# A shared tail, scaling on GpSimd and a second load behind a memset, in a ReLU-and-mean kernel

## Chip, cores and metric

The kernel runs on one core of one Trainium2 chip. The metric is the device time of one execution in microseconds (us). A time below is a median of several executions unless it says otherwise.

## The reference

```python
x = np.random.randn(32, 512, 1024).astype(np.float32)
def reference(x):
    return np.mean(np.maximum(x, 0), axis=-1).astype(np.float32)
```

There are 16,384 rows of 1024 floats (67.1 MB) to read, and one mean for each row to write (64 KB).

## The kernel before

Each of the 128 partitions holds J = 128 rows, in eight tiles of 16 rows (8.39 MB each). Three buffers take the tiles in turn. Seven tiles are loaded whole. The eighth comes in pieces of 8, 4, 2 and 1 rows, and its last row in pieces of 512, 256 and 256 columns, so that the work left over after the last bytes is small. Odd rows go to VectorE (DVE), even rows to ScalarE (ACT); each takes the ReLU and sums the row in one instruction of the kernel (1.22 us on DVE, 1.04 on ACT for 1024 columns in the trace, where the read of the accumulator follows it as an operation of its own, of 0.08 and 0.19 us).

```python
def rows(xt, lo, n, j0):
    for k in range(lo, lo + n):
        j = j0 + k
        if j % 2: dve_row(nc, xt[:, k, :], sum_v[:, j:j + 1])
        else:     act_row(nc, xt[:, k, :], sum_a[:, j:j + 1])

def finish(lo, hi):                    # scaling by 1/D, half on each engine
    nc.vector.tensor_scalar_mul(out=res[:, lo + 1:hi:2], in0=sum_v[:, lo + 1:hi:2], scalar1=inv)
    nc.scalar.mul(out=res[:, lo:hi:2], in_=sum_a[:, lo:hi:2], mul=inv)

for t in range(full):                  # full = 7
    xt = in_pool.tile([P, NB, D], F32, name="xt")
    nc.sync.dma_start(out=xt, in_=xr[:, j0:j0 + NB, :])
    rows(xt, 0, NB, j0)
# ... cut: the pieces of the eighth tile, finish() ...
act_row(nc, xt[:, lo, :D // 2], part_a[:, 0:1])          # row 14 of the last tile
dve_row(nc, xt[:, lo, D // 2:], part_v[:, 0:1])
act_row(nc, last[:, :D // 4], part_a[:, 1:2])            # row 15
dve_row(nc, last[:, D // 4:D // 2], part_v[:, 1:2])
nc.vector.tensor_scalar(...)                             # row 14: add the halves, scale
dve_row(nc, last[:, D // 2:3 * D // 4], part_v[:, 2:3])
nc.vector.tensor_scalar(...)                             # row 15: add three parts
dve_row(nc, last[:, 3 * D // 4:], part_v[:, 3:4])
nc.vector.tensor_scalar(...)                             # row 15: add the fourth, scale
nc.sync.dma_start(out=outr, in_=res)
```

Of the kernel before, what the change touches and what calls it, by code (L numbers as in the profile page):

```python
# [1 line left out]

# [4 lines left out]

F32 = mybir.dt.float32
ALU = mybir.AluOpType
RELU = mybir.ActivationFunctionType.Relu  # L10


def act_row(nc, src, acc):

    nc.scalar.activation(out=src, in_=src, func=RELU, accum_out=acc)  # L15


def dve_row(nc, src, acc):

    nc.vector.tensor_scalar(  # L20
        out=src, in0=src, scalar1=0.0, scalar2=None,
        op0=ALU.max, op1=ALU.add, accum_out=acc,
    )


@with_exitstack
def kernel(
    ctx: ExitStack,
    tc: tile.TileContext,
    x: bass.AP,  # L30
    out: bass.AP,
):
    nc = tc.nc
    P = nc.NUM_PARTITIONS
    xf = x.flatten_outer_dims()
    R, D = xf.shape
    assert R % P == 0
    J = R // P
    inv = 1.0 / D
    xr = xf.rearrange("(p j) d -> p j d", p=P, j=J)  # L40
    outr = out.flatten().rearrange("(p j) -> p j", p=P, j=J)

    NB = 16
    BUFS = 3
    full = J // NB - 1

    row_pieces = []
    left = NB
    while left > 1:
        row_pieces.append(left // 2)  # L50
        left -= left // 2
    col_pieces = [D // 2, D // 4, D // 4]

    in_pool = ctx.enter_context(tc.tile_pool(name="in", bufs=BUFS))
    res_pool = ctx.enter_context(tc.tile_pool(name="res", bufs=1))
    sum_a = res_pool.tile([P, J], F32)
    sum_v = res_pool.tile([P, J], F32)
    res = res_pool.tile([P, J], F32)
    part_a = res_pool.tile([P, 2], F32)
    part_v = res_pool.tile([P, 4], F32)  # L60

    def rows(xt, lo, n, j0):

        for k in range(lo, lo + n):
            j = j0 + k
            if j % 2:
                dve_row(nc, xt[:, k, :], sum_v[:, j:j + 1])
            else:
                act_row(nc, xt[:, k, :], sum_a[:, j:j + 1])

    def finish(lo, hi):

        nc.vector.tensor_scalar_mul(out=res[:, lo + 1:hi:2], in0=sum_v[:, lo + 1:hi:2], scalar1=inv)  # L73
        nc.scalar.mul(out=res[:, lo:hi:2], in_=sum_a[:, lo:hi:2], mul=inv)  # L74

    for t in range(full):
        j0 = t * NB
        xt = in_pool.tile([P, NB, D], F32, name="xt")
        nc.sync.dma_start(out=xt, in_=xr[:, j0:j0 + NB, :])  # L79
        rows(xt, 0, NB, j0)  # L80

    j0 = full * NB
    xt = in_pool.tile([P, NB, D], F32, name="xt")
    lo = 0
    for n in row_pieces:
        nc.sync.dma_start(out=xt[:, lo:lo + n, :], in_=xr[:, j0 + lo:j0 + lo + n, :])  # L86
        lo += n
    c = 0
    for w in col_pieces:
        nc.sync.dma_start(out=xt[:, lo, c:c + w], in_=xr[:, j0 + lo, c:c + w])  # L90
        c += w

    finish(0, j0)
    lo = 0
    for n in row_pieces[:-1]:
        rows(xt, lo, n, j0)
        lo += n
    finish(j0, j0 + lo)


    last = xt[:, NB - 1, :]
    act_row(nc, xt[:, lo, :D // 2], part_a[:, 0:1])
    dve_row(nc, xt[:, lo, D // 2:], part_v[:, 0:1])
    act_row(nc, last[:, :D // 4], part_a[:, 1:2])
    dve_row(nc, last[:, D // 4:D // 2], part_v[:, 1:2])
    nc.vector.tensor_scalar(  # L106
        out=res[:, J - 2:J - 1], in0=part_a[:, 0:1], scalar1=part_v[:, 0:1], scalar2=inv,
        op0=ALU.add, op1=ALU.mult,
    )
    dve_row(nc, last[:, D // 2:3 * D // 4], part_v[:, 2:3])  # L110
    nc.vector.tensor_scalar(  # L111
        out=part_v[:, 1:2], in0=part_v[:, 1:2], scalar1=part_a[:, 1:2], scalar2=part_v[:, 2:3],
        op0=ALU.add, op1=ALU.add,
    )
    dve_row(nc, last[:, 3 * D // 4:], part_v[:, 3:4])
    nc.vector.tensor_scalar(  # L116
        out=res[:, J - 1:J], in0=part_v[:, 3:4], scalar1=part_v[:, 1:2], scalar2=inv,
        op0=ALU.add, op1=ALU.mult,
    )
    nc.sync.dma_start(out=outr, in_=res)  # L120


# [1 line left out]
_INS = ['x']  # L124
_OUTS = [((32, 512), 'float32')]


# [23 lines left out]
```

## Time and profile before

| | before |
|---|---|
| time, median of the first 3 runs | 164.88 us |
| span in the profile | 163.1 us |
| DMA queue of the loads, share of 16 engines | 96.0% |
| DVE / ACT busy | 46% / 43% |
| first tile landed | 23.2 us |
| last piece landed | 159.19 us |
| end of DVE's last operation | 160.61 us |

A load "lands" with the last of the 16 completion marks that the trace has for it. The time from the last landing to the end of DVE's last operation I call the tail: 1.42 us here. After it come the store (1.6 us from issue to landing) and the end of the program. The views give the last landing to a tenth of a microsecond: the issue of the last piece in the timeline (its start is 120.16 us), then its size and its time from issue to landing in the DMA view. The second digit is from the marks themselves.

```profile
120.16 0.33 SPq L90 DMA_DIRECT2D xt<-in_x_dram  x1
xt<-in_x_dram SPq DMA_DIRECT2D x1, 128.0 KB, 39.0
```

Two lines of the page of the kernel before give busy shares and the chain of work that ended last:

```profile
DVE 75.4 (46%) x139; ACT 69.4 (43%) x133; POOL 0.2 (0%) x4
...
DMA 83%; DVE 14%; SPq 1%; issue 0%; DVEq 0%
```

The compute engines are idle over half of the time, and the chain is loads. The windows view of the same kernel tells why no change of compute can move much. Its columns are the stretch, its length, busy time of DVE, ACT and GpSimd (POOL), the clock, the DMA share and GB/s (a packet counts where it starts):

```profile
1.40:2.30 0.90, 0.00 (x0) 0.61 (x1) 0.00 (x0) 1.00 2.25 728
2.30:3.40 1.10, 0.00 (x0) 0.00 (x0) 0.00 (x0) 1.00 1.04 357
...
10.00:90.00 80.00, 36.25 (x63) 33.69 (x64) 0.00 (x0) 1.00 1.00 434
```

From 10 to 90 us the loads run at 434 GB/s.

The tail is read from the timeline (start, duration, engine, line, operation):

```profile
157.88 0.17 DVE L73 TENSOR_SCALAR res<-sum_v 128x7 f32<-128x7 f32 x1
157.91 0.63 ACT L15 ACTIVATE xt<-xt 128x512 f32<-128x512 f32 x1
157.96 0.68 DVE L20 TENSOR_SCALAR_CACHE_REDUCE xt<-xt 128x512 f32<-128x512 f32 x1
...
158.75 0.21 DVE L106 TENSOR_SCALAR res<-part_a,part_v 128x1 f32<-128x1 f32 x1
158.87 0.19 ACT L15 ACTIVATION_READ_ACCUMULATOR xt<-xt 128x1 f32 x1
158.88 0.41 DVE L20 TENSOR_SCALAR_CACHE_REDUCE xt<-xt 128x256 f32<-128x256 f32 x1
...
159.22 0.42 DVE L20 TENSOR_SCALAR_CACHE_REDUCE xt<-xt 128x256 f32<-128x256 f32 x1
...
159.75 0.27 DVE L111 TENSOR_SCALAR part_v<-part_v,part_a 128x1 f32<-128x1 f32 x1
159.94 0.41 DVE L20 TENSOR_SCALAR_CACHE_REDUCE xt<-xt 128x256 f32<-128x256 f32 x1
160.27 0.08 DVE L20 DVE_READ_ACCUMULATOR xt<-xt 128x1 f32 x1
160.39 0.21 DVE L116 TENSOR_SCALAR res<-part_v 128x1 f32<-128x1 f32 x1
```

ACT is done at 159.06. DVE goes on for 1.5 us, and its last piece, landed at 159.19, is not begun before 159.94. The combinations of single numbers (lines 106, 111, 116) cost 0.21 to 0.27 us each, half of a 256-column sum or more.

### The profile page before, as it was taken

The numbers are of one execution on the slowest core, as the hardware profiler recorded it, in microseconds if no ns is written. First come the engines' busy times: TensorE is split into PE (matmuls) and PEld (weight loads), VectorE is DVE, ScalarE is ACT, GpSimd is POOL, SyncE is SP. The second block draws the span as 40 slices with busy tenths as digits, with TensorE's granted clock in tenths as the row PEclk, the third lists the DMA queues.
The fourth block names the chain that finished last, engine by engine and source line by source line (L and its number), as shares of the span: only waits on it lengthen the run. The fifth ranks groups of instructions, "written<-read, shape, count | busy, mean of one in ns | idle before, by whom it ended". The sixth has DMA issues, their size and how long they took to land.

```text
span 163.1 us, 351 instructions
## 1 busy us (share of the span) xinstructions
DVE 75.4 (46%) x139; ACT 69.4 (43%) x133; POOL 0.2 (0%) x4
## 2 busy tenths in 40 slices
DVE  0000039900596008940099202990059700799993
ACT  3000039700594008920099002980059500797890
POOL 0000000000000000000000000000000000000000
DMA  7979989989998998997997998998998897999970
GB/s 257 482 321 482 482 354 450 514 354 418 514 418 354 514 418 354 514 482 305 498 484 340 466 498 354 434 514 370 402 514 386 386 514 338 434 442 394 409 298 16
DMA packets 2162, 67.19 MB, mean 412 GB/s; under 512 B 240, under 2 KB 624, under 8 KB 880
## 3 DMA queue, kind: packets, MB, share of 16 engines
q1 hardware_dynamic: 2160, 67.18, 96.0%
q14 instruction: 2, 0.02, 0.0%
HBM read 67.11 MB, written 0.07 MB: 412 GB/s over the span
## 4 chain that ended last, share of the span: by engine, by line
DMA 83%; DVE 14%; SPq 1%; issue 0%; DVEq 0%
DMA xt<-in_x_dram 83%; DVE xt L20 13%; SPq L86 0%; SPq L79 0%; DVE part_v L111 0%; DVE res L116 0%; DVE res L106 0%; DVE res L73 0%; DVEq L20 0%; DVEq L111 0%; DVEq L106 0%
## 5 line engine op out<-in xcount | busy, mean ns | idle before, releaser
L20 DVE TENSOR_SCALAR_CACHE_REDUCE xt<-xt 128x1024 f32<-128x1024 f32 (+1 forms) x67 | 74.4, 1172 | 84.9 <-DMA xt<-in_x_dram 84.8
L15 ACT ACTIVATE xt<-xt 128x1024 f32<-128x1024 f32 (+1 forms) x65 | 66.7, 1027 | 88.9 <-DMA xt<-in_x_dram 88.9
L15 ACT ACTIVATION_READ_ACCUMULATOR xt<-xt 128x1 f32 x65 | 12.1, 187 | 0.0
L20 DVE DVE_READ_ACCUMULATOR xt<-xt 128x1 f32 x67 | 5.6, 83 | 0.0
L15 ACT ACT_TABLE_LOAD x1 | 1.3, 1283 | 0.7 <-PEq L135 0.7
L74 ACT ACTIVATE res<-sum_a 128x56 f32<-128x56 f32 (+1 forms) x2 | 0.5, 232 | 0.1
L73 DVE TENSOR_SCALAR res<-sum_v 128x56 f32<-128x56 f32 (+1 forms) x2 | 0.4, 184 | 0.1
L111 DVE TENSOR_SCALAR part_v<-part_v,part_a 128x1 f32<-128x1 f32 x1 | 0.3, 273 | 0.1
L106 DVE TENSOR_SCALAR res<-part_a,part_v 128x1 f32<-128x1 f32 x1 | 0.2, 214 | 0.1
L116 DVE TENSOR_SCALAR res<-part_v 128x1 f32<-128x1 f32 x1 | 0.2, 214 | 0.0
L135 POOL MEMSET const-uint8-127<- 128x1 uint8 x1 | 0.1, 102 | 0.0
L135 POOL MEMSET const-bfloat16-1.0<- 128x1 bf16 x1 | 0.1, 101 | 0.0
L135 POOL MEMSET const-float32-0.0<- 128x1 f32 x1 | 0.1, 98 | 0.2 <-issue 0.2
L135 POOL MEMSET const-float32-1.0<- 128x1 f32 x1 | 0.1, 98 | 0.0
## 6 DMA issues: line engine op xcount, KB each, us to landing
xt<-in_x_dram SPq DMA_DIRECT2D x1, 4096.0 KB, 39.0
xt<-in_x_dram SPq DMA_DIRECT2D x1, 2048.0 KB, 43.5
xt<-in_x_dram SPq DMA_DIRECT2D x1, 1024.0 KB, 45.5
xt<-in_x_dram SPq DMA_DIRECT2D x1, 512.0 KB, 46.3
xt<-in_x_dram SPq DMA_DIRECT2D x1, 256.0 KB, 46.5
xt<-in_x_dram SPq DMA_DIRECT2D x2, 128.0 KB, 42.7
xt<-in_x_dram SPq DMA_DIRECT2D x7, 48.9
out_dram<-res SPq DMA_DIRECT2D x1, 64.0 KB, 1.6
```

What stands on the lines that cost most here:

```text
L15: nc.scalar.activation(out=src, in_=src, func=RELU, accum_out=acc)
L20: nc.vector.tensor_scalar(out=src, in0=src, scalar1=0.0, scalar2=None, op0=ALU.max, op1=ALU.add, accum_out=acc,)
L73: nc.vector.tensor_scalar_mul(out=res[:, lo + 1:hi:2], in0=sum_v[:, lo + 1:hi:2], scalar1=inv)
L74: nc.scalar.mul(out=res[:, lo:hi:2], in_=sum_a[:, lo:hi:2], mul=inv)
L106: nc.vector.tensor_scalar(out=res[:, J - 2:J - 1], in0=part_a[:, 0:1], scalar1=part_v[:, 0:1], scalar2=inv, op0=ALU.add, op1=ALU.mult,)
L111: nc.vector.tensor_scalar(out=part_v[:, 1:2], in0=part_v[:, 1:2], scalar1=part_a[:, 1:2], scalar2=part_v[:, 2:3], op0=ALU.add, op1=ALU.add,)
L116: nc.vector.tensor_scalar(out=res[:, J - 1:J], in0=part_v[:, 3:4], scalar1=part_v[:, 1:2], scalar2=inv, op0=ALU.add, op1=ALU.mult,)
L135: nc = _bacc.Bacc("TRN2", target_bir_lowering=False, num_devices=1)
```

## The change

It wants to shorten the tail and to order the start. (1) The scaling and the combination of row 14 go to GpSimd. (2) In the third quarter of row 15, ACT takes 128 columns. DVE's last two sums take the sum before them as start value instead of being added later, and ACT folds in its own parts while DVE works on the last piece. (3) The second load is issued only after GpSimd has set two rows of its buffer to zero. The core of the diff (cut: names, constants, the merging of the sum tiles):

```diff
-def dve_row(nc, src, acc):
+def dve_row(nc, src, acc, init=None):
-        out=src, in0=src, scalar1=0.0, scalar2=None,
+        out=src, in0=src, scalar1=0.0, scalar2=init,
...
-        nc.vector.tensor_scalar_mul(out=res[:, lo + 1:hi:2], ...)
-        nc.scalar.mul(out=res[:, lo:hi:2], ...)
+        nc.gpsimd.tensor_scalar(out=res[:, lo:hi], in0=sums[:, lo:hi], scalar1=inv, scalar2=0.0, ...)
...
+        if t == 1:
+            nc.gpsimd.memset(xt[:, 0:2, :], 0.0)
...
-    nc.vector.tensor_scalar(out=res[:, J - 2:J - 1], ...)
+    nc.gpsimd.tensor_scalar(out=res[:, J - 2:J - 1], ...)
-    dve_row(nc, last[:, D // 2:3 * D // 4], part_v[:, 2:3])
-    nc.vector.tensor_scalar(out=part_v[:, 1:2], ...)
-    dve_row(nc, last[:, 3 * D // 4:], part_v[:, 3:4])
-    nc.vector.tensor_scalar(out=res[:, J - 1:J], ...)
+    nc.gpsimd.tensor_scalar(out=part[:, 4:5], in0=part[:, 2:3], scalar1=inv, ...)
+    act_row(nc, last[:, 512:640], part[:, 5:6])
+    dve_row(nc, last[:, 640:768], part[:, 6:7], init=part[:, 3:4])
+    nc.scalar.activation(out=part[:, 7:8], in_=part[:, 5:6], func=ACT.Identity, scale=inv, bias=part[:, 4:5])
+    dve_row(nc, last[:, 768:], part[:, 8:9], init=part[:, 6:7])
+    nc.vector.scalar_tensor_tensor(out=res[:, J - 1:J], in0=part[:, 8:9], scalar=inv, in1=part[:, 7:8], ...)
```

More of the change, by code (lines that the diff above doesn't have):

```diff
@@ L9 @@
 ALU = mybir.AluOpType
-RELU = mybir.ActivationFunctionType.Relu
+ACT = mybir.ActivationFunctionType
 def act_row(nc, src, acc):
-    nc.scalar.activation(out=src, in_=src, func=RELU, accum_out=acc)
-def dve_row(nc, src, acc):
+    nc.scalar.activation(out=src, in_=src, func=ACT.Relu, accum_out=acc)
+def dve_row(nc, src, acc, init=None):
     nc.vector.tensor_scalar(
-        out=src, in0=src, scalar1=0.0, scalar2=None,
+        out=src, in0=src, scalar1=0.0, scalar2=init,
         op0=ALU.max, op1=ALU.add, accum_out=acc,
@@ L41 @@
     outr = out.flatten().rearrange("(p j) -> p j", p=P, j=J)
+    xlast = xr[:, J - 1, :]
     NB = 16
-    BUFS = 3
     full = J // NB - 1
-    row_pieces = []
-    left = NB
-    while left > 1:
-        row_pieces.append(left // 2)
-        left -= left // 2
-    col_pieces = [D // 2, D // 4, D // 4]
-    in_pool = ctx.enter_context(tc.tile_pool(name="in", bufs=BUFS))
+    row_pieces = [8, 4, 2, 1]
+    assert sum(row_pieces) == NB - 1
+    col_pieces = [512, 256, 256]
+    assert sum(col_pieces) == D
+    in_pool = ctx.enter_context(tc.tile_pool(name="in", bufs=3))
     res_pool = ctx.enter_context(tc.tile_pool(name="res", bufs=1))
-    sum_a = res_pool.tile([P, J], F32)
-    sum_v = res_pool.tile([P, J], F32)
+    sums = res_pool.tile([P, J], F32)
     res = res_pool.tile([P, J], F32)
-    part_a = res_pool.tile([P, 2], F32)
-    part_v = res_pool.tile([P, 4], F32)
+    part = res_pool.tile([P, 10], F32)
     def rows(xt, lo, n, j0):
@@ L65, in rows @@
             j = j0 + k
-            if j % 2:
-                dve_row(nc, xt[:, k, :], sum_v[:, j:j + 1])
-            else:
-                act_row(nc, xt[:, k, :], sum_a[:, j:j + 1])
+            (dve_row if j % 2 else act_row)(nc, xt[:, k, :], sums[:, j:j + 1])
     def finish(lo, hi):
-        nc.vector.tensor_scalar_mul(out=res[:, lo + 1:hi:2], in0=sum_v[:, lo + 1:hi:2], scalar1=inv)
-        nc.scalar.mul(out=res[:, lo:hi:2], in_=sum_a[:, lo:hi:2], mul=inv)
+        nc.gpsimd.tensor_scalar(
+            out=res[:, lo:hi], in0=sums[:, lo:hi], scalar1=inv, scalar2=0.0, op0=ALU.mult, op1=ALU.add,
+        )
     for t in range(full):
@@ L83 @@
     xt = in_pool.tile([P, NB, D], F32, name="xt")
+    prev, last = xt[:, NB - 2, :], xt[:, NB - 1, :]
     lo = 0
@@ L89 @@
     for w in col_pieces:
-        nc.sync.dma_start(out=xt[:, lo, c:c + w], in_=xr[:, j0 + lo, c:c + w])
+        nc.sync.dma_start(out=last[:, c:c + w], in_=xlast[:, c:c + w])
         c += w
@@ L98 @@
     finish(j0, j0 + lo)
-    last = xt[:, NB - 1, :]
-    act_row(nc, xt[:, lo, :D // 2], part_a[:, 0:1])
-    dve_row(nc, xt[:, lo, D // 2:], part_v[:, 0:1])
-    act_row(nc, last[:, :D // 4], part_a[:, 1:2])
-    dve_row(nc, last[:, D // 4:D // 2], part_v[:, 1:2])
-    nc.vector.tensor_scalar(
-        out=res[:, J - 2:J - 1], in0=part_a[:, 0:1], scalar1=part_v[:, 0:1], scalar2=inv,
-        op0=ALU.add, op1=ALU.mult,
-    )
-    dve_row(nc, last[:, D // 2:3 * D // 4], part_v[:, 2:3])
-    nc.vector.tensor_scalar(
-        out=part_v[:, 1:2], in0=part_v[:, 1:2], scalar1=part_a[:, 1:2], scalar2=part_v[:, 2:3],
-        op0=ALU.add, op1=ALU.add,
-    )
-    dve_row(nc, last[:, 3 * D // 4:], part_v[:, 3:4])
-    nc.vector.tensor_scalar(
-        out=res[:, J - 1:J], in0=part_v[:, 3:4], scalar1=part_v[:, 1:2], scalar2=inv,
-        op0=ALU.add, op1=ALU.mult,
+    act_row(nc, prev[:, :512], part[:, 0:1])
+    dve_row(nc, prev[:, 512:], part[:, 1:2])
+    nc.gpsimd.tensor_scalar(
+        out=res[:, J - 2:J - 1], in0=part[:, 0:1], scalar1=part[:, 1:2], scalar2=inv, op0=ALU.add, op1=ALU.mult,
+    )
+    act_row(nc, last[:, :256], part[:, 2:3])
+    dve_row(nc, last[:, 256:512], part[:, 3:4])
+    nc.gpsimd.tensor_scalar(
+        out=part[:, 4:5], in0=part[:, 2:3], scalar1=inv, scalar2=0.0, op0=ALU.mult, op1=ALU.add,
+    )
+    act_row(nc, last[:, 512:640], part[:, 5:6])
+    dve_row(nc, last[:, 640:768], part[:, 6:7], init=part[:, 3:4])
+    nc.scalar.activation(
+        out=part[:, 7:8], in_=part[:, 5:6], func=ACT.Identity, scale=inv, bias=part[:, 4:5],
+    )
+    dve_row(nc, last[:, 768:], part[:, 8:9], init=part[:, 6:7])
+    nc.vector.scalar_tensor_tensor(
+        out=res[:, J - 1:J], in0=part[:, 8:9], scalar=inv, in1=part[:, 7:8], op0=ALU.mult, op1=ALU.add,
     )
```

## The prediction

> **What bounds the kernel now.** The load stream. The page gives DMA 96% of 16 engines' span, DVE 46%, ACT 43%; the chain of waits is 83% DMA, 14% DVE. From issue times plus issue-to-landing times, the seven full tiles land at 23.2, 42.5, ... 139.6 us, one per 19.3 to 19.4 us; 8.39 MB in 19.35 us is 433 GB/s. [...] What can move is the start (issue 0.73, first landing 23.2: about 3 us more than a steady tile) and the tail.
>
> **Tail before (timeline).** The last pieces land at about 156.6 (rows 12, 13), 157.8 (row 14), 158.5, 158.85 and 159.16 us (row 15). DVE, not the last load, ends the chain: row 13 from 156.62, scaling 157.88, half row, 158.75 combination (0.21), 256 columns at 158.88 and 159.22, combination of 0.27, 256 columns at 159.94, last combination 160.39 to 160.60. Then the store (1.6 us) and the end.
>
> **What the change does to the tail.** It takes the scaling (0.17) and two combinations (0.21, 0.27) off DVE and gives 128 of its columns to ACT (a 256-column op costs DVE 0.41, ACT 0.42; 512 columns 0.68 and 0.63; so I estimate 128 columns at 0.28 and 0.31). In exchange two DVE ops now take the preceding DVE sum as their start value: each waits for the accumulator read and a semaphore (0.11 us gap, as the trace shows before the 0.27 us combination) and carries a pointer operand (+0.04 to 0.06, from 0.21 and 0.27 against 0.17). My schedule: half row to 158.5; 256 columns from 158.56 (their landing); 128 from 159.1; last 256 from 159.55 to 160.0; final op 160.13 to 160.4. DVE gains only about 0.2 us. ACT: 128 columns to 159.4, then Identity; it needs a GpSimd product that can start at about 159.15. [...] no table load; the trace's ACT scaling after Relu has none either. GpSimd has about 0.5 us before it delays DVE; no GpSimd arithmetic is in the trace, only 0.1 us memsets, so this is my weakest size.
>
> **What the memset does.** 128x2048 floats on GpSimd[...] hold loads 2 and 3 back [...]. Load 1 occupies the engines until about 21 us, so nothing starves. In the trace eight engines' first packets start at 1.6 to 2.1 us, the other eight only at 2.4 to 3.0, after issue of load 2 at 1.16, and this stagger survives to the end. If the second issue causes it, delaying it brings the late engines forward by up to 0.8 us, and all landings with them. I give that less than even odds: worth 0.2 us in the mean.
>
> **Sum.** 164.88 - 0.2 (tail) - 0.2 (start) = 164.45 us. Range 163.7 to 165.2. Faster by over 2% would need 3.3 us, more than tail and start hold; slower by over 2% needs a table load plus slow GpSimd ops.
>
> **What would show it.** Landings still 19.3 to 19.4 us apart; first landing 23.2 (no effect) or 22.4 to 23.0 (stagger gone); no second table load; DVE's last op ending 1.2 us after the last landing instead of 1.44; [...] loads 2, 3 issued behind it.
>
> **What would make it wrong.** GpSimd ops of 1 us or more, making the last combination wait for ACT's Identity, or the store for GpSimd; a larger gain at the start; the delayed issue slowing the stream, for instance if loads must be queued early to follow on without a gap; the pointer start value costing DVE more than I took.

Sum: it takes 0.2 us for the tail and 0.2 us for the start off 164.88 us and was put at 164.45 us (164.48 without a slip).

## The result and the profile after

The changed kernel took 164.81 us (median of 4 runs, 164.4 to 164.86) beside 164.94 us for the kernel before (4 runs). The ratio is 0.9984, with a 95% interval of 0.9964 to 1.0004. A ratio here and below is the mean time of one kernel's fast runs over that of the kernel before in the same rounds, so it is not quite the ratio of the medians. With more rounds the changed kernel came out at 0.9976 (0.9959 to 0.9994), so it is about 0.4 us faster (0.1 to 0.7 us by the interval).

The page after, the same two lines:

```profile
DVE 74.7 (46%) x135; ACT 69.6 (43%) x134; POOL 3.0 (2%) x9
...
DMA 83%; DVE 13%; POOL 1%; SPq 1%; issue 0%; DVEq 0%; POOLq 0%
```

The loads are still the chain. The 1% of POOL in it is the memset at the start, through which the trace now leads back to the second load. The windows of the same stretches:

```profile
1.40:2.30 0.90, 0.00 (x0) 0.61 (x1) 0.90 (x1) 1.00 2.25 728
2.30:3.40 1.10, 0.00 (x0) 0.00 (x0) 0.24 (x1) 1.00 0.99 357
...
10.00:90.00 80.00, 36.16 (x63) 33.70 (x64) 0.00 (x0) 1.00 1.01 434
```

Again ten first packets start before 2.3 us and six after it, and the rate is the same 434 GB/s. The tail in the timeline after:

```profile
158.33 0.69 DVE L20 TENSOR_SCALAR_CACHE_REDUCE xt<-xt 128x512 f32<-128x512 f32 x1
158.43 0.22 POOL L65 TENSOR_SCALAR res<-sums 128x14 f32<-128x14 f32 x1 [8.71 <-DVE xt L20]
...
158.96 0.42 DVE L20 TENSOR_SCALAR_CACHE_REDUCE xt<-xt 128x256 f32<-128x256 f32 x1
159.20 0.27 POOL L101 TENSOR_SCALAR res<-part 128x1 f32<-128x1 f32 x1 [0.55 <-ACT xt L15]
...
159.31 0.08 DVE L20 DVE_READ_ACCUMULATOR xt<-xt 128x1 f32 x1
...
159.43 0.35 DVE L20 TENSOR_SCALAR_CACHE_REDUCE xt<-xt,part 128x128 f32<-128x128 f32 x1
159.55 0.19 POOL L106 TENSOR_SCALAR part<-part 128x1 f32<-128x1 f32 x1
...
159.81 0.48 DVE L20 TENSOR_SCALAR_CACHE_REDUCE xt<-xt,part 128x256 f32<-128x256 f32 x1
159.86 0.29 ACT L111 ACTIVATE part<-part 128x1 f32<-128x1 f32 x1
160.22 0.08 DVE L20 DVE_READ_ACCUMULATOR xt<-xt,part 128x1 f32 x1
160.41 0.16 DVE L115 SCALAR_TENSOR_TENSOR res<-part 128x1 f32<-128x1 f32 x1
```

The same two views of the last piece after:

```profile
120.57 0.33 SPq L87 DMA_DIRECT2D xt<-in_x_dram  x1
xt<-in_x_dram SPq DMA_DIRECT2D x1, 128.0 KB, 39.0
```

In this trace the last piece landed at 159.60 us, 0.41 us later than in the trace of before, and DVE ended at 160.57, 0.04 us earlier. So the tail fell from 1.42 to 0.97 us, and nearly all of that gain is hidden by a later landing. Either the memset caused the later landing, or it was chance.

### The profile page after: what moved, and what is told of

It reads as the page before. It is cut to its first block, busy times and chain, and to the rows that moved or that the text cites. A ratio compares the mean times of both kernels' runs of the same rounds, so it can differ in the third digit from the quotient of the medians.

```text
span 163.1 us, 361 instructions
## 1 busy us (share of the span) xinstructions
DVE 74.7 (46%) x135; ACT 69.6 (43%) x134; POOL 3.0 (2%) x9
## 4 chain that ended last, share of the span: by engine, by line
DMA 83%; DVE 13%; POOL 1%; SPq 1%; issue 0%; DVEq 0%; POOLq 0%
DMA xt<-in_x_dram 83%; DVE xt L20 12%; POOL xt L74 1%; SPq L83 1%; DVE res L115 0%; DVEq L20 0%; SPq L75 0%; DVEq L115 0%; POOLq L133 0%
## 5 line engine op out<-in xcount | busy, mean ns | idle before, releaser
L65 POOL TENSOR_SCALAR res<-sums 128x112 f32<-128x112 f32 (+1 forms) x2 | 0.5, 254 | 155.6 <-DVE xt L20 155.6
L74 POOL MEMSET xt<- 128x2048 f32 x1 | 1.8, 1805 | 0.3 <-POOLq L133 0.3
L20 DVE TENSOR_SCALAR_CACHE_REDUCE xt<-xt,part 128x128 f32<-128x128 f32 (+1 forms) x2 | 0.8, 412 | 0.1
```

The costliest lines, as they stand in the source:

```text
L20: nc.vector.tensor_scalar(out=src, in0=src, scalar1=0.0, scalar2=init, op0=ALU.max, op1=ALU.add, accum_out=acc,)
L65: nc.gpsimd.tensor_scalar(out=res[:, lo:hi], in0=sums[:, lo:hi], scalar1=inv, scalar2=0.0, op0=ALU.mult, op1=ALU.add,)
L74: nc.gpsimd.memset(xt[:, 0:2, :], 0.0)
```

## The experiments

Theory H1 was: the tail is worth 0.45 us, the memset nothing, and the later landing of the one trace is chance. The rival H2 was: holding the second load back makes the stream end later and eats the gain. The first four runs separate the parts of the change, beside a control, on one chip.

### Control: the kernel before, unchanged

> A null control: the kernel before, unchanged. 164.9 us, ratio 1.000 within 0.001 under every theory. It gives the spread that a difference of 0.3 us has to stand out from. In its trace: where the last load lands (159.2 us in the first trace of before) and how far apart the 16 completions of one load lie (0.95 us, then 1.17 us after about 90 us). If the last landing moves by 0.3 us or more here, landings of one trace can't be read as an effect of the change.

Measured: 165.15 us (6 runs), ratio 0.9996 (0.9977 to 1.0015). Its last landing was at 159.65 us, against 159.19 in the first trace of the same program. So a landing in one trace varies by 0.46 us with nothing changed. That is as much as the difference that H2 was built on. Its tail was 1.43 us. The 16 completion marks of one load lay 0.90 and 0.87 us apart for its first two tiles, 1.21 us from the third on and 1.75 us from the fifth on. Both steps are tiles that landed late, 19.73 and 19.87 us after the tile before.

### The changed kernel again

> The changed kernel again. Theory H1 (the tail is 0.45 us shorter, the memset worth nothing, and the later last landing of its first trace, 159.6 against 159.2 us, was chance): about 164.5 us, ratio 0.997 to 0.998. Rival H2 (the held-back second load makes the stream end 0.4 us later and eats the tail's gain): ratio 0.9985 to 1.000, and the last landing again at about 159.6 us.

Measured: 164.72 us (6 runs), ratio 0.9976 (0.9959 to 0.9994), last landing 159.30 us, tail 0.97 us. The landing did not repeat at 159.6, against H2.

### The memset alone

```diff
         xt = in_pool.tile([P, NB, D], F32, name="xt")
+        if t == 1:
+            nc.gpsimd.memset(xt[:, 0:2, :], 0.0)
         nc.sync.dma_start(out=xt, in_=xr[:, j0:j0 + NB, :])
```

> The kernel before with only the memset of the second buffer. H1: ratio 1.000, no effect beyond the control's spread. H2: 165.3 us, ratio 1.002 to 1.003, last landing about 159.6 us. Under both the second load is issued at about 2.55 us in place of 1.16.

Measured: 165.09 us (5 runs), ratio 1.0001 (0.9982 to 1.002), last landing 159.23 us, tail 1.43 us. The memset alone is worth nothing that these rounds can see. H1 holds so far.

### The tail alone

```diff
-        if t == 1:
-            nc.gpsimd.memset(xt[:, 0:2, :], 0.0)
```

> The changed kernel without the memset: only the tail. H1: the same as the changed kernel, ratio 0.997 to 0.998. H2: faster than the changed kernel by 0.3 to 0.4 us, ratio 0.9965 to 0.9975 while the changed kernel is at 0.9985 to 1.000. Under both, DVE's last operation ends about 0.97 us after the last landing, against 1.42 us before.

Measured: 164.54 us (5 runs), ratio 0.9967 (0.9949 to 0.9986), tail 0.97 us. Its interval overlaps that of the changed kernel (0.9959 to 0.9994), so it can't be ranked against it. Together with the run before, this puts the gain in the tail. H2 falls: the memset alone did not come out at 1.002 to 1.003 (its interval just reaches 1.002), and in three more traces with a held load (the changed kernel again, the memset alone, the hold below) the last piece landed at 159.2 to 159.3 us and not at 159.6. A cost of 0.1 or 0.2 us of the memset is not excluded by these times.

### Holding the second load eight times as long

```diff
-            nc.gpsimd.memset(xt[:, 0:2, :], 0.0)
+            nc.gpsimd.memset(xt, 0.0)
```

> The changed kernel with the memset over the whole second buffer, 8 times the work: by the 1.805 us measured for one eighth it should take 14.4 us and hold load 2 back to about 15.2 us. H1 (a held-back load costs nothing while the load before it still feeds the DMA engines): time unchanged, 164.3 to 164.9 us, first landing 23.1 us and 19.3 to 19.5 us between landings. Rival (loads must be queued early, or any hold costs some of the stream): slower by 0.5 us or more, with the gap between the first and the second landing above 19.5 us.

Measured: 164.52 us (4 runs), ratio 0.9964 (0.995 to 0.9977). The timeline has the memset and the two loads held behind it (SPq is the DMA issue of SyncE):

```profile
0.73 13.75 POOL L74 MEMSET xt<- 128x16384 f32 x1 [0.29 <-POOLq L133]
...
14.51 0.81 SPq L75 DMA_DIRECT2D xt<-in_x_dram  x2
```

The second load is issued 13.35 us later than in the kernel before (1.16 us), and the second landing comes 19.31 us after the first, as before. A load held while another still ran cost nothing here.

### Holding it twice as long again

```diff
             nc.gpsimd.memset(xt, 0.0)
+            nc.gpsimd.memset(xt, 0.0)
```

> The changed kernel with that whole-buffer memset twice: load 2 issued at about 29.6 us, after load 1 has landed at 23.1. Under H1 this is where the hold must start to cost: the second landing comes the first load's own 22.4 us after the issue, at about 52.0 us in place of 42.4, and the whole program is 9.5 us longer, about 174 us (173 to 175). If the time moves by much less than 8 us, I have the order of the loads or their queueing wrong.

My expectation failed: 164.66 us (4 runs), ratio 0.9973 (0.9958 to 0.9988). The trace shows why. Two loads were issued at once (0.74 and 1.16 us) and only the third waited for GpSimd, until 28.32 us. In the built program the unheld load stands ahead of the held one; I take this to be the work of the tile scheduler, which no run tested. The held load was not needed before the second landing at 42.6 us. This run says nothing of a hold beyond the first load's end, so the experiment was built anew.

### Holding loads 2 and 3 beyond the end of load 1

```diff
+    scr = res_pool.tile([P, 2048], F32)
+    for _ in range(15):
+        nc.gpsimd.memset(scr, 0.0)
...
-        if t == 1:
-            nc.gpsimd.memset(xt[:, 0:2, :], 0.0)
+        if t in (1, 2):
+            nc.gpsimd.tensor_copy(out=xt[:, 0, 0:1], in_=scr[:, 0:1])
```

> The changed kernel with loads 2 and 3 both held back behind 15 GpSimd memsets of 128x2048 on a scratch tile (a one-column copy from that tile into each buffer makes the dependence): load 2 issued at about 28.5 to 29.5 us, 5 to 6 us after load 1 has landed. The run with two memsets on one buffer did not do this, since the tile scheduler moved the third load ahead of the held one. H1: now the DMA engines stand idle from about 22 to 30 us, the second landing comes 21.3 to 22.4 us after the issue, at 50 to 52 us in place of 42.45, and all that follows is 8 to 9.5 us later: 172.5 to 174 us. Rival (the stream catches up later): less than 168 us.

Measured: 173.61 us (4 runs), ratio 1.0511. The windows show the hole in the stream (last column GB/s), and the waits of the DMA issue name GpSimd:

```profile
20.00:23.00 3.00, 0.00 (x0) 0.00 (x0) 2.94 (x2) 1.00 0.20 87
23.00:30.00 7.00, 6.92 (x13) 6.92 (x13) 5.73 (x6) 1.00 0.18 56
30.00:40.00 10.00, 2.28 (x5) 1.50 (x4) 0.00 (x0) 1.00 0.92 380
```

```profile
SPq L78 <- POOL xt L77: 27.9, 1, 27.9
```

The issue came at 28.87 us and the second landing 28.10 us after the first instead of 19.3. Nothing of these 8.8 us is caught up later: the time is 8.9 us over the 164.72 us of the changed kernel (on another chip). So the changed kernel's hold to 2.56 us is free because the first load keeps the DMA engines fed until about 22 us (in this trace the last of its packets start at 20.3 us and end at 22.7 us). If a later issue costs one for one, 28.87 less 8.8 puts the limit of a free hold near 20 us; that is an estimate from this one run.

### Which part of the tail gained

Two builds add the parts of the new tail to the kernel before, one after the other. First the scaling on GpSimd:

```diff
-        nc.vector.tensor_scalar_mul(out=res[:, lo + 1:hi:2], ...)
-        nc.scalar.mul(out=res[:, lo:hi:2], ...)
+        for first, s in ((lo, sum_a), (lo + 1, sum_v)):
+            nc.gpsimd.tensor_scalar(out=res[:, first:hi:2], in0=s[:, first:hi:2], scalar1=inv, ...)
```

> The kernel before with only the final scaling (the two operations of 0.17 and 0.21 us at rows 112 to 125) moved to GpSimd. I read the tail in the trace, since its length from the last landing to the end of DVE's last operation came out the same within 0.02 us in every run so far: 1.42 to 1.43 us before, 0.97 to 0.99 after. DVE's half row started 0.08 us after row 14 landed because of the scaling, so I expect 1.35 us (1.30 to 1.43). If the scaling were the larger part of the gain, the tail would be near 1.1 us.

Measured: tail 1.38 us (one run of 165.01 us). Then also the combination of row 14:

```diff
-    nc.vector.tensor_scalar(out=res[:, J - 2:J - 1], ...)
+    nc.gpsimd.tensor_scalar(out=res[:, J - 2:J - 1], ...)
```

> The kernel before with the scaling and the combination of row 14 (0.21 us of DVE plus its waits) moved to GpSimd; row 15 still done as before. Without the combination DVE should start the third quarter of row 15 about 0.3 us earlier, so the tail should be 1.05 us (1.0 to 1.15), nearly all of the gain. If instead the shared columns and the chained start values of row 15 are what gained, it stays at 1.25 us or more.

Measured: tail 1.11 us (one run of 165.1 us, with its last landing at 159.71 us, 0.5 us later than in the first trace of before, so its time is not to be compared). The steps are 1.42, 1.38, 1.11 and 0.97 us: scaling 0.04, the combination of row 14 0.27, and the new order of row 15 0.14 us. Each step is one trace, and the parts of the last one (columns shared with ACT, start values, the part that ACT folds in) were not separated. The timeline shows what the second step did; DVE goes straight from one 256-column sum to the next while GpSimd combines:

```profile
159.07 0.42 DVE L20 TENSOR_SCALAR_CACHE_REDUCE xt<-xt 128x256 f32<-128x256 f32 x1
159.32 0.27 POOL L109 TENSOR_SCALAR res<-part_a,part_v 128x1 f32<-128x1 f32 x1 [0.47 <-ACT xt L15]
...
159.42 0.42 DVE L20 TENSOR_SCALAR_CACHE_REDUCE xt<-xt 128x256 f32<-128x256 f32 x1
```

### More of row 15 on GpSimd

```diff
-    dve_row(nc, last[:, 640:768], part[:, 6:7], init=part[:, 3:4])
-    nc.scalar.activation(out=part[:, 7:8], ..., func=ACT.Identity, ...)
-    dve_row(nc, last[:, 768:], part[:, 8:9], init=part[:, 6:7])
-    nc.vector.scalar_tensor_tensor(out=res[:, J - 1:J], ...)
+    dve_row(nc, last[:, 640:768], part[:, 6:7])
+    nc.gpsimd.tensor_scalar(out=part[:, 7:8], in0=part[:, 5:6], scalar1=part[:, 6:7], scalar2=part[:, 4:5], ...)
+    dve_row(nc, last[:, 768:], part[:, 8:9])
+    nc.vector.tensor_scalar(out=res[:, J - 1:J], in0=part[:, 8:9], scalar1=part[:, 7:8], scalar2=inv, ...)
```

(The GpSimd product before it, in place of the scaling by 1/D, adds the two first quarters.)

> The changed kernel without the memset and without the chained start values: the four earlier partial sums of row 15 are added on GpSimd, in two operations, and DVE's last operations take no start value. The chained last piece took 0.48 us where 256 columns took 0.42 us before, and it started 0.2 us after its data had landed. I expect it to start within 0.05 us of the landing and the tail to be 0.86 us (0.80 to 0.95), unless GpSimd's second sum ends later than DVE's last row piece; then DVE waits for GpSimd and the tail is 0.97 us or more. By time 164.5 us, ratio 0.996 to 0.9975: not to be told from the changed kernel.

Measured: 164.73 us (6 runs), ratio 0.9976 (0.9961 to 0.9991), tail 0.97 us. It was the second branch of the expectation:

```profile
159.47 0.42 DVE L20 TENSOR_SCALAR_CACHE_REDUCE xt<-xt 128x256 f32<-128x256 f32 x1
159.81 0.36 POOL L108 TENSOR_SCALAR part<-part 128x1 f32<-128x1 f32 x1
159.82 0.08 DVE L20 DVE_READ_ACCUMULATOR xt<-xt 128x1 f32 x1
160.20 0.21 DVE L112 TENSOR_SCALAR res<-part 128x1 f32<-128x1 f32 x1 [0.30 <-POOL part L108]
```

DVE's last sum now starts 0.02 us after the landing (159.45) and is 0.06 us shorter without a start value. But then DVE waits 0.30 us for GpSimd, whose sum of three single numbers takes 0.36 us. What was taken from DVE came back as a wait. The changed kernel stays clear of this: there DVE's last read ends at 160.30, after ACT's Identity at 160.15.

### Why the landings vary: dummy operations

In each of the 13 traces without dummies, two 8 KB packets of the instruction queue share the DMA engines with the loads in the middle of the stream. In eleven of them they lie at 85.0 to 87.8 us, and one tile then lands late: the gap from tile 3 to tile 4 (counted from 0) is 19.53 to 20.02 us, where the others are 19.3 to 19.5, but for one: the control also has 19.73 us at tile 2, with no such packet near it. In the other two, with loads 2 and 3 held back and with two queues (below), the loads run 9 and 20 us later, and so do the packets (96 and 105 to 107 us). Theory R says these are instructions that DVE and ACT will need next, fetched after a number of instructions. The test runs 28 tiny operations on each before the first landing, in the kernel without the memset:

```diff
+    junk = res_pool.tile([P, 8], F32)
+    junk_acc = res_pool.tile([P, 64], F32)
+    nc.vector.memset(junk, 0.0)
+    for i in range(28):
+        dve_row(nc, junk[:, 0:2], junk_acc[:, i:i + 1])
+        act_row(nc, junk[:, 4:6], junk_acc[:, 32 + i:33 + i])
```

> The changed kernel without the memset, with 28 tiny dummy operations on DVE and on ACT before the first load lands, where both engines are idle. In each trace so far two 8 KB packets of the instruction queue are in the DMA engines at 85 to 87.5 us, when DVE and ACT are at about their 28th row, and the gap between the landings of tiles 3 and 4 (ending about 101 us) is 19.57 to 19.89 us where the others are 19.3 to 19.5. Theory R (these are the next instructions of DVE and ACT, fetched when they have run so many[...]): the two packets move to the first 25 us, the gap at tile 4 falls to 19.35, and the loss shows in the first or second landing or disappears; time within 0.4 us of the kernel without dummies. Rival R2 (the packets come at a fixed time or byte count, or the longer gap at tile 4 is not theirs): packets and gap stay at 85 to 101 us.

The DMA view of the control for 84 to 88 us has the two packets (queue, kind, packets, MB, share):

```profile
q1 hardware_dynamic: 29, 1.90, 110.1%
q14 instruction: 2, 0.02, 1.0%
```

With the dummies that stretch has none:

```profile
q1 hardware_dynamic: 29, 1.90, 109.6%
```

They are at 9 to 14 us instead, and two more appear at 152 to 155 us. DVE's first operation on tiles 3 and 4 shows the gap; first the control, then the kernel with dummies:

```profile
81.55 1.22 DVE L20 TENSOR_SCALAR_CACHE_REDUCE xt<-xt 128x1024 f32<-128x1024 f32 x1 [10.29 <-DMA xt<-in_x_dram]
101.42 1.22 DVE L20 TENSOR_SCALAR_CACHE_REDUCE xt<-xt 128x1024 f32<-128x1024 f32 x1 [10.66 <-DMA xt<-in_x_dram]
```

```profile
81.72 1.22 DVE L20 TENSOR_SCALAR_CACHE_REDUCE xt<-xt 128x1024 f32<-128x1024 f32 x1 [10.26 <-DMA xt<-in_x_dram]
101.07 1.22 DVE L20 TENSOR_SCALAR_CACHE_REDUCE xt<-xt 128x1024 f32<-128x1024 f32 x1 [10.15 <-DMA xt<-in_x_dram]
```

The gap fell from 19.87 to 19.35 us, so packets and loss moved with the number of instructions run, and R2 falls. With the dummies the completion marks of a load lie 1.34 to 1.36 us apart from the first tile on, without a step at tile 4. How two packets of 0.31 us each delay a tile by 0.2 to 0.7 us is not shown. The first landing came later (23.51 against 23.0 to 23.3 us), as expected. The time did not fit: 165.39 us (5 runs), ratio 1.0018 (1.0005 to 1.003), where I had expected at most 0.4 us over 164.54. I had not reckoned with a second pair of packets. It came in the middle of the last pieces, and the last one landed 40.0 us after its issue instead of 39.0. The 1.0 us is lost between the landings of the first and the second piece (149.34 and 155.30 us, 5.96 us apart instead of 4.89), where these packets lie; no run took them away alone. That the packets hold instructions is told by the name of their queue in the trace alone; whether one is DVE's and the other ACT's was not tried.

### The first load on two queues

```diff
+        if t == 0:
+            nc.sync.dma_start(out=xt[:P // 2], in_=xr[:P // 2, j0:j0 + NB, :])
+            nc.scalar.dma_start(out=xt[P // 2:], in_=xr[P // 2:, j0:j0 + NB, :])
+        else:
+            nc.sync.dma_start(out=xt, in_=xr[:, j0:j0 + NB, :])
```

> The changed kernel without the memset, with the first load split in two: partitions 0 to 63 issued by SP, 64 to 127 by ACT. In every trace so far half of the engines' first packets start at about 1.6 to 2.2 us and the rest at 2.4 to 3.1. Theory S ([...] half of the engines start late, and the stream keeps that stagger): with two queues the late half starts up to 0.6 us earlier, first landing at about 22.6 us and last landing some 0.3 to 0.5 us earlier: about 164.1 us. Rival S2 (the split costs as much, by a later start of ACT's queue or worse spread over the engines): first landing 23.1 us or later, 164.5 us or more.

Measured: 184.45 us (4 runs), ratio 1.1174, first landing 43.23 us (SP's half at 43.06, ACT's at 43.23). Both theories missed by far. The rate halves until 40 us, in the windows view:

```profile
5.00:40.00 35.00, 0.00 (x0) 0.00 (x0) 0.00 (x0) 1.00 0.98 210
45.00:90.00 45.00, 24.93 (x45) 24.54 (x48) 0.00 (x0) 1.00 0.97 419
```

The DMA view shows the two queues in turn: 16 packets of one start in each 5 us, first SP's (q1, 0 to 5 us), then ACT's (q10, 5 to 10 us):

```profile
q1 hardware_dynamic: 16, 1.05, 95.5%
```

```profile
q10 hardware_dynamic: 16, 1.05, 97.7%
```

Packets of 64 KB take 4.9 us instead of 2.42. Why is not shown: no run separates the split by partitions from the second queue.

## Why the prediction was right, point by point

The measured 164.81 us is inside the range of 163.7 to 165.2, at 0.36 us from the forecast of 164.45. The forecast is a gain of 0.26%; the changed kernel measured 0.16% and 0.24% in its two comparisons. Its two terms were not right in size, and that their sum came so close is luck: the tail gave 0.25 us more than forecast, the start 0.2 us less, and the two errors cancel. The range also holds 164.88 us, so to lie inside it does not tell a gain from none. (The sum has a slip: 164.88 - 0.2 - 0.2 is 164.48.)

- **"The load stream" bounds the kernel: right as far as tested.** The rate was 434 GB/s before and after, and the only run that put a hole into the stream (hold to 28.87 us) lost all of it. That the middle of the stream cannot shrink was not shown: no run tried to raise the rate.
- **"DVE gains only about 0.2 us" in the tail: the mechanism was right, the size too small.** It measured 0.45 us (1.42 to 0.97). I charged a 0.11 us wait before each sum with a start value, read from a combination that also waits for ACT. In the trace after, such a sum starts 0.04 us after the accumulator read before it ends (159.39 to 159.43, and again 159.77 to 159.81). And I gave the last combination 0.27 us; it took 0.16. Two times 0.07 and 0.11 are 0.25 us, which is the difference. The cost of a start value (0.04 to 0.06) was right: 0.48 against 0.42 us. Most of the gain, 0.27 us, is one combination of single numbers taken off DVE in the middle of the tail.
- **The memset "worth 0.2 us in the mean": wrong, no gain was seen.** The part of the step that failed is "If the second issue causes it", to which I had given less than even odds. The time of the memset alone (1.0001, 0.9982 to 1.002) would not exclude 0.2 us; the traces say more. With the second load issued at 2.56, 14.51 or 28.87 us, 9 to 11 of the 16 first packets start before 2.3 us and the rest after; with it issued at 1.16 us it is 6 to 11. So the stagger stays. The first landing does not follow it either: 23.05 to 23.11 us with the hold, 22.96 to 23.26 without (runs without dummies, on one queue). Its description was off too: ten and six engines in the trace that I read, not eight and eight. The hold of loads 2 and 3 (by a memset of 1.80 us, issued at 2.56 and 2.94 us) and "nothing starves" were right.
- **No table load, GpSimd within about 0.5 us: right.** Identity ran with no second load (the trace after has one ACT_TABLE_LOAD, at 0.73 us). GpSimd's single-number operations took 0.19 to 0.27 us, and the run with more on GpSimd, where they took 0.26 to 0.36 us and DVE waited 0.30 us, shows how near that limit is.
- **"Landings still 19.3 to 19.4 us apart": not quite.** One gap per run, at the instruction packets, is 19.5 to 20.0 us in both kernels. It moves the last landing by up to 0.5 us from run to run, as much as the whole gain. Of the 0.41 us by which the first trace after landed later, 0.32 us lie in this gap (19.89 against 19.57 us), so one trace of each kernel seemed to show that the gain was eaten. The late tile 2 of the control (19.73 us, no packets) has another cause, which stays open.

No version tried is faster than the changed kernel clear of the noise. Without the memset it is simpler and no slower (0.9967).

## What to carry to other kernels

Here loads bounded the kernel, and the tail is the part that the change of compute shortened (1.42 to 0.97 us). Take operations on single numbers off the engine that ends the chain (one combination less on DVE was 0.27 us of it), but check that the engine that gets them is not then the last (with more on GpSimd, DVE waited 0.30 us). A queued load that was issued late cost nothing while the load before it still fed the DMA engines (an issue at 14.51 us was free, where that load landed at 23.1 us); issued 5.8 us after that landing, it cost 8.8 us. A landing seen in one trace moved by 0.46 us with nothing changed, so compare lengths that repeat, such as the time from the last landing to the last operation (1.42 and 1.43 us in two traces of the kernel before), and run a control.
